# Layer 0's later modulation starts with the mLSTM's weights; each half's sum is taken ahead of the next half

## The chip, the core and the metric

The kernel runs on one core of a Trainium2 chip. The metric is the device time of one execution in microseconds; before the change it is 1823.27 us, the median of three runs. The core's engines are named as the profile names them: PE is TensorE's matrix multiply, PEld its weight load, DVE VectorE, ACT ScalarE, POOL GpSimd, SP SyncE, whose queue issues the loads.

## What is computed

Two layers of a diffusion trunk on 256 latent tokens and 256 context tokens of width 1024. In each layer an adaLN modulation (six vectors of 1024 per side, from `SiLU(c)` and `SiLU(c_ctx)`) acts on the normed input; one projection feeds four mixers side by side (A: HGRN2 recurrence, B: mLSTM, C: grouped-query attention, D: latent attention); their outputs are gated, summed, projected out and added; then comes a squared-ReLU MLP, modulated too. Cut to that:

```python
for l in range(DEPTH):
    mod = jnp.split((s_c @ w_ada[l] + b_ada[l])[:, None, :], 6, axis=-1)
    mod_c = jnp.split(s_cc @ w_ada[l][:, :n_cm * D_MODEL] + b_ada[l][:n_cm * D_MODEL], n_cm)
    h_l = modulate(rms_norm(x_l, g_norm1[l]), mod[0], mod[1])       # h_c with mod_c
    p_l = h_l @ w_in[l]
    ...   # ya: hgrn2, yb: mlstm, yc: gqa, yd: mla, latent reads context too
    x_l = x_l + mod[2] * (merge_branches((ya_l, yb_l, yc_l, yd_l), lat['gates'], w_branch[l]) @ w_out[l])
    x_l = x_l + mod[5] * squared_relu_mlp(modulate(rms_norm(x_l, g_norm2[l]), mod[3], mod[4]), w_ff1[l], w_ff2[l])
    ...   # the context side likewise in layer 0
return rms_norm(x_l, g_final)
```

## The kernel before

**Weights.** Every big weight comes in blocks of 128 x 1024 f32 (512 KB). `plan` writes a list of them (`specs`) in the order of use; `get` hands out the next and, by `_prep`, loads and splits one block ahead. A block is loaded into one of three buffers (`raw`), then ScalarE writes its rounded high part (`whi`, line 139) and VectorE the rest (`wlo`, line 140), each from a pool of two. A product takes three matmuls, high by high, high by low, low by high; a block is 24 matmuls of 512 columns. They go into PSUM tiles `pd`. All other matmuls, those of the recurrences and attentions, go into four PSUM buffers `pm`.

**Modulation.** The first two of layer 0's six vectors are made at the start (`ada_start`, names `ad`). The other four are two groups of 2048 columns (`ada_specs(0, 1)` and `(0, 2)`), each in two halves of eight blocks: 32 chunks. A chunk is not split. VectorE multiplies it by the side's conditioning value and adds it to an accumulator of 128 x 1024, once for each of the two sides (lines 390 and 392). After the eighth chunk of a half, `ada_sum` sums the accumulators over partitions with matmuls (line 404), copies the row (line 407, ScalarE), transposes it (line 263) and adds the bias (line 414). It is called at the next `get` of a split block at which the half is one block old, or at once with `now=True`; `mixer_b` has such a call ahead of its state C. The accumulators, C, the attentions' probabilities and queries share the pool `w4` of four buffers of 4 KB per partition.

**What sets the order.** `fill` holds the chunks that wait; `plan` puts one behind each split block while there are any. `ORDER[0]` sets the units: `A` (three weights for each of three heads, the first head's come at the start), `RA` (A's readout, 4 blocks), `B` (12 blocks; `mixer_b` makes gates and state), `b` (one mLSTM head of one side; four context heads, then four latent ones), `M0` (a quarter of a branch merge, 3 blocks), `CD` (queries for C and D, 6 blocks), `RB`, `C`, and so on. A scheduler then sets each engine's queue, by priority in the order of the program, as buffers come free. A queue runs in order.

**The recurrences.** A head of A has eight levels: ScalarE copies K, TensorE multiplies (line 636), VectorE multiplies K and Q by F (lines 654, 658), F by itself (662) and picks results (663). A head of B: scores (line 865), then for each of two directions a row matmul (870), VectorE (876, 879), ScalarE's exponential (881) and decay (889), VectorE (882, 883, 890), the product with values and state (900); then the norm (904 to 906) and the output (909, 910). Behind and between these stand the matmuls of weight blocks, named filling below.

Of the kernel before, what the change touches and what calls it, by code (L numbers as in the profile page):

```python
# [40 lines left out]
class Trunk:  # L41
# [337 lines left out]
    def ada_chunk(self, key):  # L379

        nc = self.nc
        _, l, g, k, jj = key
        raw, _ = self.get(key)
        sides = (0, 1) if l == 0 or g == 0 else (0,)
        if k == 0:
            self.ada_acc = [self.t("w4", [128, 1024], name=f"aacc{g}{jj}{r}") for r in sides]
        for r in sides:
            acc, s = self.ada_acc[r], self.scol[:, k, r:r + 1]
            if k == 0:
                nc.vector.tensor_scalar(out=acc, in0=raw, scalar1=s, scalar2=None, op0=ALU.mult)  # L390
            else:
                nc.vector.scalar_tensor_tensor(out=acc, in0=raw, scalar=s, in1=acc, op0=ALU.mult, op1=ALU.add)  # L392
        if k == KT - 1:
            self.pending = (l, g, jj, sides, self.ada_acc, self.next_use + 1)
# [632 lines left out]
    def mixer_c(self, l):  # L1027
        nc = self.nc
        need = l == 0
        i0 = 0 if need else 2  # L1030
        q0 = i0 * 128
        KVD, QS, R = self.KVD, self.QS, self.CDR
        kn = self.t("w2", [128, 4, 128], name=f"ckn{l}")
        for i in range(4):
            kv = kn[:, i, :].rearrange("p (h c) -> p h c", h=2)
            nc.vector.scalar_tensor_tensor(out=kv, in0=KVD[:, i, 16:144].rearrange("p (h c) -> p h c", h=2), scalar=0.125,
                                           in1=R[:, i, 8:10].unsqueeze(2).to_broadcast([128, 2, 64]), op0=ALU.mult, op1=ALU.mult)
            if i < 2:
                nc.vector.tensor_tensor(out=kv, in0=kv, in1=self.gain[:, l * 2 + 1, :].unsqueeze(1).to_broadcast([128, 2, 64]), op=ALU.mult)
            else:  # L1040
                tmp = self.t("w2", [128, 512])[:, 0:128].rearrange("p (h c) -> p h c", h=2)
                self.rope(tmp, kv, self.rt[:, l * 2 + 1, 0, i - 2, :], self.rt[:, l * 2 + 1, 1, i - 2, :], 2, nc.vector)
                nc.vector.tensor_scalar(out=kv, in0=tmp, scalar1=1.0, scalar2=None, op0=ALU.mult)
        for i in range(i0, 4):
            qv = QS[:, i, :].rearrange("p (h c) -> p h c", h=8)
            nc.vector.tensor_tensor(out=qv, in0=qv, in1=R[:, i, 0:8].unsqueeze(2).to_broadcast([128, 8, 64]), op=ALU.mult)
            if i < 2:
                nc.vector.tensor_tensor(out=qv, in0=qv, in1=self.gain[:, l * 2, :].unsqueeze(1).to_broadcast([128, 8, 64]), op=ALU.mult)
            else:
                tmp = self.t("w2", [128, 512])  # L1050
                self.rope(tmp.rearrange("p (h c) -> p h c", h=8), qv, self.rt[:, l * 2, 0, i - 2, :], self.rt[:, l * 2, 1, i - 2, :], 8, nc.vector)
                nc.vector.tensor_copy(QS[:, i, :], tmp)
        ps = self.pm()
        for i in range(4):
            self.tr(ps[:, i * 128:(i + 1) * 128], kn[:, i, :])
        ks = [self.dup_key(ps, g * 64, f"ck{l}{g}") for g in range(2)]
        Y = self.t("b16", [128, 2, 4, 512], F32R, name=f"yc{l}")
        yield Y
        for pp in range(2):
            Ts = []  # L1060
            for kvh in range(2):
                ps = self.pm()
                for i in range(i0, 4):
                    c0 = (kvh * 4 + pp * 2) * 64
                    self.tr(ps[:, i * 128:(i + 1) * 128], QS[:, i, c0:c0 + 128])
                Ts.append(self.split_pair(ps, q0))
            for gg in range(2):
                g4 = pp * 2 + gg
                pts = {}
                for sd in range(i0 // 2, 2):  # L1070
                    ns = 256 if sd == 0 else 512
                    for kvh in range(2):
                        PT = pts[kvh, sd] = self.t("w4", [128, 4, 256])
                        for tt in range(2):
                            i = 2 * sd + tt
                            pss = self.pm()
                            self.score64(pss[:, 0:ns], Ts[kvh][gg], slice(i * 128, (i + 1) * 128), ks[kvh], ns, True, True)
                            self.softmax_t(pss[:, 0:ns], ns, PT[:, 0:ns // 128, tt * 128:(tt + 1) * 128])

                def values(g4=g4, pts=pts):  # L1080
                    po = self.pm()
                    for sd in range(i0 // 2, 2):
                        nst = 2 if sd == 0 else 4
                        for st in range(nst):
                            for kvh in range(2):
                                nc.tensor.matmul(po[kvh * 64:(kvh + 1) * 64, sd * 256:(sd + 1) * 256],  # L1086
                                                 KVD[:, st, 144 + kvh * 64:144 + (kvh + 1) * 64], pts[kvh, sd][:, st, :],
                                                 start=(st == 0), stop=(st == nst - 1), skip_group_check=True)
                    nc.scalar.activation(out=Y[:, 0, g4, q0:], in_=po[:, q0:], func=AF.Copy)
                    nc.vector.tensor_tensor(out=Y[:, 1, g4, q0:], in0=po[:, q0:], in1=Y[:, 0, g4, q0:].bitcast(F32), op=ALU.subtract)  # L1090

                self.later.append((0, values))
                if g4 == 3:
                    self.run_later()
                yield
# [263 lines left out]
    def run(self):  # L1359
        nc = self.nc  # L1360
        for l in range(2):
            if l == 0:
                self.plan_start()
                self.fill += self.ada_specs(0, 1) + self.ada_specs(0, 2)
            m = [0] * 4
            for u in ORDER[l].split():
                if u == "A":
                    self.plan_a(l)
                elif u == "RA":
                    self.plan_tmw(("ag", l), l, O_AG)  # L1370
                elif u == "B":
                    self.plan_b(l)
                elif u == "CD":
                    self.plan_cd(l)
                elif u == "RB":
                    self.plan_tmw(("bo", l), l, O_BO)
                elif u[0] == "M":
                    r = int(u[1])
                    self.plan_merge(l, r, (m[r],))
                    m[r] += 1  # L1380
            self.plan_out(l)
            if l == 0:
                self.fill += self.ada_specs(1, 0) + self.ada_specs(1, 1) + self.ada_specs(1, 2)
            self.plan_ff(l)
# [136 lines left out]
```

## Time and profile before

| | |
|---|---|
| median of 3 runs | 1823.27 us (1821.34 to 1823.35) |
| the profiled execution | 1824.29 us, its span 1822.5 us |
| TensorE busy | 1772.4 us, 97% |
| VectorE busy | 1201.3 us, 66% |
| ScalarE busy | 834.6 us, 46% |
| loads | 228.80 MB, mean 129 GB/s |

A record of a matmul lasts from its start to a modelled end, and the next starts well before that end; so the spacing of starts tells TensorE's rate, and idle time is what lies between one record's end and the next start. The granted clock (PEclk) is a share of 2.4 GHz. A row of the timeline may merge equal instructions, with their count behind x; in brackets stands the idle time of the engine just before, and what ended it. A matmul of plain f32 operands shows as two records.

### The profile page before, as it was taken

Reading aid. Unit: us, or ns where it says so; the run is one execution under the profiler, and the core shown is the slowest. Engines: PE = TensorE matmul, PEld = TensorE weight load, DVE = VectorE, ACT = ScalarE, POOL = GpSimd, SP = SyncE. Lnnn points to the kernel's source line nnn. Section 1 sums busy time; section 2 is a strip of 40 time slices with the busy share of each in tenths; the row PEclk is TensorE's granted clock in tenths of the full one; section 3 lists DMA queues with packets and bytes.
Section 4 is the critical chain, followed back from the end, with each engine's and each line's share of the span. In section 5 each row is a group of like instructions: output and inputs, shape, how many; then the busy total and the mean of one; then the engine's idle time right before and its main releaser. Section 6 shows DMA issues by size and latency. Waiting matters only on the chain.

```text
span 1822.5 us, 26354 instructions
## 1 busy us (share of the span) xinstructions
PE 1772.4 (97%) x10214; PEld 1496.8 (82%) x10214; DVE 1201.3 (66%) x2047; ACT 834.6 (46%) x1481; POOL 122.3 (7%) x139
## 2 busy tenths in 40 slices
PE   7999899999999999999999999999999999989998
PEld 5788777888767778897888888888789779989998
DVE  5798798647754444579884435587666965656665
ACT  4443343354653333443433334443455664545555
POOL 0000000000001111010101010000000001001110
PEclk9999899999999999999999999999999999999999
DMA  9643245223112234337783234222335425545554
GB/s 292 195 122 107 70 139 178 86 87 93 47 36 77 73 120 123 105 114 222 242 288 105 93 95 145 72 74 62 93 116 168 139 70 151 156 134 160 181 183 137
DMA packets 210045, 234.71 MB, mean 129 GB/s; under 512 B 8320, under 2 KB 186880, under 8 KB 209664
## 3 DMA queue, kind: packets, MB, share of 16 engines
q1 hardware_dynamic: 209920, 233.03, 42.2%
q8 instruction: 80, 1.31, 0.3%
q14 instruction: 45, 0.37, 0.1%
HBM read 228.80 MB, written 4.19 MB: 128 GB/s over the span
## 4 chain that ended last, share of the span: by engine, by line
PE 83%; DVE 9%; issue 3%; ACT 3%; DMA 2%; SPq 0%; POOL 0%; ACTq 0%; DVEq 0%; POOLq 0%
PE pd L198 14%; PE pd L196 14%; PE pd L197 14%; PE pd L168 4%; PE pd L167 4%; PE pd L169 4%; PE pd L238 3%; PE pd L239 3%; PE pd L240 3%; PE pm L263 3%; PE pm L636 2%; DVE wlo L140 2%; PE pm L900 1%; DVE aacc L392 1%; PE pm L1086 1%
## 5 line engine op out<-in xcount | busy, mean ns | idle before, releaser
L140 DVE TENSOR_TENSOR wlo<-raw,whi 128x1024 fp32r<-128x1024 f32 (+1 forms) x305 | 384.7, 1262 | 275.9 <-ACT whi L139 273.8
L139 ACT ACTIVATE whi<-raw 128x1024 fp32r<-128x1024 f32 (+1 forms) x305 | 321.6, 1056 | 401.6 <-PE pd L197 180.4
L198 PE MATMUL pd<-HH,wlo 128*128 128x256 f32 (+1 forms) x1104 | 371.2, 337 | 2.7 <-DVE wlo L140 2.6
L196 PE MATMUL pd<-HH,whi 128*128 128x256 f32 (+1 forms) x1104 | 372.1, 337 | 0.0
L197 PE MATMUL pd<-HL,whi 128*128 128x256 f32 (+1 forms) x1104 | 370.2, 335 | 0.0
L198 PEld LDWEIGHTS pd<-HH,wlo 128*128 128x128 f32 x1104 | 209.4, 190 | 25.3 <-DVE wlo L140 4.9
L196 PEld LDWEIGHTS pd<-HH,whi 128*128 128x128 f32 x1104 | 209.5, 190 | 22.0 <-issue 1.5
L197 PEld LDWEIGHTS pd<-HL,whi 128*128 128x128 f32 x1104 | 209.6, 190 | 20.3 <-issue 0.5
L196 PE MATMUL pd<-b,whi 128*128 128x256 f32 (+1 forms) x528 | 175.5, 332 | 0.0
L198 PE MATMUL pd<-b,wlo 128*128 128x256 f32 (+1 forms) x528 | 175.2, 332 | 0.2 <-DVE wlo L140 0.2
L197 PE MATMUL pd<-b,whi 128*128 128x256 f32 (+1 forms) x528 | 175.4, 332 | 0.0
L238 PE MATMUL pd<-whi,HH 128*128 128x512 f32 (+1 forms) x272 | 107.9, 397 | 2.3 <-DVE d L712 1.0
L196 PEld LDWEIGHTS pd<-b,whi 128*128 128x128 f32 x528 | 100.3, 190 | 10.5 <-issue 0.8
L198 PEld LDWEIGHTS pd<-b,wlo 128*128 128x128 f32 x528 | 100.3, 190 | 10.3 <-DVE wlo L140 1.0
L197 PEld LDWEIGHTS pd<-b,whi 128*128 128x128 f32 x528 | 100.3, 190 | 9.4 <-DVE b L1347 0.2
L239 PE MATMUL pd<-whi,HL 128*128 128x512 f32 (+1 forms) x272 | 106.4, 391 | 0.0
L240 PE MATMUL pd<-wlo,HH 128*128 128x512 f32 (+1 forms) x272 | 104.4, 391 | 0.5 <-DVE wlo L140 0.5
L434 ACT ACTIVATE w<-X 128x256 f32<-128x256 f32 x120 | 47.5, 411 | 104.4 <-DVE X L1243 104.4
L169 PE MATMUL pd<-HH,wlo 128*128 128x512 f32 (+1 forms) x232 | 87.6, 378 | 4.6 <-DVE wlo L140 4.6
L1236 POOL TENSOR_TENSOR mg<-mg,d 128x512 f32<-128x512 f32 (+1 forms) x48 | 53.4, 1114 | 555.4 <-DVE d L1235 540.4
L1346 POOL TENSOR_TENSOR d<-d 128x256 f32<-128x256 f32 (+1 forms) x60 | 56.5, 946 | 492.6 <-ACT b L1344 477.8
L168 PE MATMUL pd<-HL,whi 128*128 128x512 f32 (+1 forms) x232 | 87.6, 377 | 0.0
(422 smaller groups left out, 3306.8 us busy)
## 6 DMA issues: line engine op xcount, KB each, us to landing
raw<-in_w_in_dram SPq DMA_DIRECT2D x140, 512.0 KB, 3.7
raw<-in_w_ff_dram SPq DMA_DIRECT2D x128, 512.0 KB, 3.7
w<-in_w_ada_dram SPq DMA_DIRECT2D x48, 512.0 KB, 5.0
raw<-in_w_ada_dram SPq DMA_DIRECT2D x32, 512.0 KB, 3.8
raw<-in_w_branch_dram SPq DMA_DIRECT2D x24, 512.0 KB, 3.5
raw<-in_w_out_dram SPq DMA_DIRECT2D x16, 512.0 KB, 3.5
w<-in_w_ada_dram SPq DMA_DIRECT2D x28, 256.0 KB, 5.5
raw<-in_w_branch_dram SPq DMA_DIRECT2D x16, 256.0 KB, 4.0
```

The costliest lines, as they stand in the source:

```text
L139: nc.scalar.activation(out=hi[:, 0:n], in_=raw[:, 0:n], func=AF.Copy)
L140: nc.vector.tensor_tensor(out=lo[:, 0:n], in0=raw[:, 0:n], in1=hi[:, 0:n].bitcast(F32), op=ALU.subtract)
L167: nc.tensor.matmul(out, lh, rh, start=(i == 0), stop=False)
L168: nc.tensor.matmul(out, lh, rl, start=False, stop=False)
L169: nc.tensor.matmul(out, ll, rh, start=False, stop=(i == n - 1))
L196: nc.tensor.matmul(o, wh, act[0], start=(k == 0), stop=False, skip_group_check=True)
L197: nc.tensor.matmul(o, wh, act[1], start=False, stop=False, skip_group_check=True)
L198: nc.tensor.matmul(o, wl, act[0], start=False, stop=(k == KT - 1), skip_group_check=True)
L238: nc.tensor.matmul(o, hh, wh, start=(k == 0), stop=False, skip_group_check=True)
L239: nc.tensor.matmul(o, hl, wh, start=False, stop=False, skip_group_check=True)
L240: nc.tensor.matmul(o, hh, wl, start=False, stop=(k == KT - 1), skip_group_check=True)
L1346: eng.tensor_tensor(out=r, in0=r, in1=r, op=ALU.mult)
```

## The change

The 32 chunks of layer 0 are put on `fill` ahead of unit `B` and no longer ahead of unit `A`. So A's nine weight blocks and RA's four have no chunk between them, and the chunks stand behind the blocks of B, of three quarters of the merge, of CD and of RB. At the first chunk of a half `ada_sum(True)` now takes the sum of the half before, and so does the head of `mixer_c`.

```diff
@@ -383,6 +383,7 @@
         if k == 0:
+            self.ada_sum(True)
             self.ada_acc = [self.t("w4", [128, 1024], name=f"aacc{g}{jj}{r}") for r in sides]
@@ -1030,6 +1031,7 @@
         KVD, QS, R = self.KVD, self.QS, self.CDR
+        self.ada_sum(True)
         kn = self.t("w2", [128, 4, 128], name=f"ckn{l}")
@@ -1361,7 +1363,6 @@
             if l == 0:
                 self.plan_start()
-                self.fill += self.ada_specs(0, 1) + self.ada_specs(0, 2)
             m = [0] * 4
@@ -1369,6 +1370,9 @@
                 elif u == "B":
+                    if l == 0:
+
+                        self.fill += self.ada_specs(0, 1) + self.ada_specs(0, 2)
                     self.plan_b(l)
```

Line numbers of the changed kernel are one higher behind line 385, two higher behind line 1033.

VectorE's queue in the first head of A, before (`ah` is the head's K, Q and F, `w2` the result, `aacc` an accumulator, `raw30` a chunk):

```order
L392 SCALAR_TENSOR_TENSOR aacc100_814<-raw30_1038,scol_112,aacc100_814 128x1024
L654 TENSOR_TENSOR ah00_680<-ah00_680 128x2x64x4
L658 TENSOR_TENSOR ah00_680<-ah00_680 128x2x64x4
L663 COPY_PREDICATED w2_96_690<-lmask_647,pm_100_719 128x512
L662 TENSOR_TENSOR ah00_680<-ah00_680 128x128
L140 TENSOR_TENSOR wlo29_888<-raw29_885,whi29_887 128x1024
L654 TENSOR_TENSOR ah00_680<-ah00_680 128x2x32x8
L658 TENSOR_TENSOR ah00_680<-ah00_680 128x2x32x8
L663 COPY_PREDICATED w2_96_690<-lmask_647,pm_101_729 128x512
L662 TENSOR_TENSOR ah00_680<-ah00_680 128x64
L392 SCALAR_TENSOR_TENSOR aacc101_815<-raw30_1038,scol_112,aacc101_815 128x1024
```

The same levels after:

```order
L655 TENSOR_TENSOR ah00_680<-ah00_680 128x2x64x4
L659 TENSOR_TENSOR ah00_680<-ah00_680 128x2x64x4
L663 TENSOR_TENSOR ah00_680<-ah00_680 128x128
L655 TENSOR_TENSOR ah00_680<-ah00_680 128x2x32x8
L659 TENSOR_TENSOR ah00_680<-ah00_680 128x2x32x8
L664 COPY_PREDICATED w2_96_690<-lmask_647,pm_101_729 128x512
L663 TENSOR_TENSOR ah00_680<-ah00_680 128x64
L140 TENSOR_TENSOR wlo26_876<-raw26_873,whi26_875 128x1024
```

The sums over chunks are gone from between the levels, and weights are split less far ahead. The first chunk's sum (L391) now stands in the fourth head.

TensorE's queue in the mLSTM's latent heads, from one direction's product to the next head's row matmul, before (`pm` are PSUM tiles of the recurrence, `pd` of the weights, `C0` the state):

```order
L900 MATMUL pm_314_2654<-bv0_2119,w2_312_2644 128x129 x2
L865 MATMUL pm_316_2669<-w2_232_2095,w2_226_2009 128x256
L900 MATMUL pm_314_2654<-C0_2288,w2_313_2650 128x129
L900 MATMUL pm_314_2654<-bv0_2119,w2_312_2644 128x129
L900 MATMUL pm_314_2654<-C0_2288,w2_313_2650 128x129
L865 MATMUL pm_316_2669<-w2_232_2095,w2_226_2009 128x256
L870 MATMUL pm_317_2672<-nM0_1908,rsel_101 128x256
L198 MATMUL pd_343_2878<-HH_125,wlo87_2884 128x512
L196 MATMUL pd_343_2878<-HH_125,whi87_2883 128x512
L197 MATMUL pd_343_2878<-HL_126,whi87_2883 128x512
```

After, from the row matmul of the third latent head on:

```order
L871 MATMUL pm_307_2584<-nM0_1836,rsel_101 128x256
L901 MATMUL pm_310_2596<-bv0_2031,w2_308_2586 128x129
L871 MATMUL pm_311_2602<-nM0_1836,rsel_101 128x256
L901 MATMUL pm_310_2596<-C0_2200,w2_309_2592 128x129
L901 MATMUL pm_310_2596<-bv0_2031,w2_308_2586 128x129 x2
L901 MATMUL pm_310_2596<-C0_2200,w2_309_2592 128x129
L901 MATMUL pm_314_2614<-bv0_2031,w2_312_2604 128x129
L866 MATMUL pm_316_2629<-w2_222_2007,w2_216_1921 128x256
L901 MATMUL pm_314_2614<-bv0_2031,w2_312_2604 128x129
L901 MATMUL pm_314_2614<-C0_2200,w2_313_2610 128x129
```

Before, 19 such matmuls on weights follow the row matmul shown, and 24 stand within each latent head; after, six stand in the second latent head and none from there to the end of the fourth. Weights follow behind it, six blocks in a row.

VectorE's queue at the end of the fourth latent head, after (`bden` is the head's norm, `bh0` its output, `mod0` the modulation):

```order
L891 TENSOR_TENSOR w2_323_2658<-w2_323_2658,w2_222_2007 64x256
L391 TENSOR_SCALAR aacc201_2738<-raw69_2713,scol_112 128x1024
L906 TENSOR_TENSOR bden_325_2668<-bden_325_2668,bEM_228_2026 128x4
L393 SCALAR_TENSOR_TENSOR aacc201_2738<-raw71_2769,scol_112,aacc201_2738 128x1024
L907 RECIPROCAL bden_325_2668<-bden_325_2668 128x4
L415 TENSOR_TENSOR mod0_103<-pm_330_2732,PT_107 128x2x4 x2
L1235 SCALAR_TENSOR_TENSOR mg0_2300<-d2_333_2765,pd_335_2779 128x512
L911 SCALAR_TENSOR_TENSOR bh0_2227<-pm_324_2662,bden_325_2668,bh0_2227 128x128 x2
L1235 SCALAR_TENSOR_TENSOR mg0_2300<-d2_334_2767,pd_336_2793 128x512
L393 SCALAR_TENSOR_TENSOR aacc201_2738<-raw73_2809,scol_112,aacc201_2738 128x1024
L699 TENSOR_REDUCE cdst_356_3203<-w2_359_3211 128x4
L140 TENSOR_TENSOR wlo74_2814<-raw74_2811,whi74_2813 128x1024
```

The last group's second accumulator (`aacc201`) is first written here, some 80 rows behind its first (`aacc200`), from the chunks `raw69`, `raw71` and `raw73`; the next weight split is `wlo74`. Before, the accumulators of every half are written side by side.

## Rows read from the trace of the kernel before

**Rows 1.** The page's head: span, and each engine's busy time.
```profile
span 1822.5 us, 26354 instructions
PE 1772.4 (97%) x10214; PEld 1496.8 (82%) x10214; DVE 1201.3 (66%) x2047; ACT 834.6 (46%) x1481; POOL 122.3 (7%) x139
```

**Rows 2.** Stretches: length, busy us (instructions) by engine, PEclk, loads' share, GB/s.
```profile
core 0: us, PE busy (x) PEld busy (x) DVE busy (x) ACT busy (x) POOL busy (x), PEclk, DMA share, GB/s
160.00:180.00 20.00, 18.64 (x116) 15.99 (x115) 16.89 (x25) 7.39 (x12) 0.59 (x2) 1.00 0.32 95
180.00:200.00 20.00, 15.98 (x92) 13.28 (x90) 20.00 (x32) 5.68 (x9) 0.00 (x0) 0.95 0.36 106
200.00:220.00 20.00, 16.38 (x91) 14.34 (x92) 12.76 (x23) 8.79 (x15) 1.57 (x3) 0.79 0.24 73
...
240.00:260.00 20.00, 17.33 (x76) 13.39 (x75) 19.65 (x32) 9.17 (x13) 0.00 (x0) 1.00 0.31 91
...
280.00:300.00 20.00, 18.60 (x117) 13.48 (x117) 15.29 (x24) 6.98 (x12) 0.00 (x0) 1.00 0.63 186
...
400.00:420.00 20.00, 20.00 (x106) 17.21 (x105) 14.78 (x36) 12.79 (x30) 0.00 (x0) 1.00 0.35 104
...
1220.00:1240.00 20.00, 19.86 (x125) 17.20 (x124) 16.94 (x37) 8.02 (x17) 1.15 (x2) 1.00 0.26 71
```

**Rows 3.** Eight stretches from 60 to 220 us, instructions on accumulators alone, summed.
```profile
sum 160.00, PE 1.07 PEld 0.42 DVE 39.56; mean PE 0.13 PEld 0.05 DVE 4.94
```

**Rows 4.** Line 392, layer 0: count, shortest, median and longest ns, first and last.
```profile
L392 DVE SCALAR_TENSOR_TENSOR aacc<-raw,scol,aacc x56: 1265/1276/1292, 72.2 to 325.7; 128x1024 f32<-128x1024 f32 x56
```

**Rows 5.** Timeline of TensorE, end of HGRN2's last head: start, us, instruction, idle before.
```profile
193.90 1.16 PE L636 MATMUL pm<-ah 128*128 128x128 f32 x8 [1.35 <-ACT ah L632]
196.44 1.16 PE L645 MATMUL pm<-ah 128*128 128x128 f32 x8 [1.38 <-DVE ah L658]
198.67 1.11 PE L263 MATMUL pm<-cst,ah 128*128 128x128 f32 x4 [1.07 <-DVE ah L654]
...
209.61 0.44 PE L263 MATMUL pm<-cst,arow 128*128 128x128 f32 x2 [2.17 <-ACT arow L407]
```

**Rows 6.** Stretches ahead of and in the first fall of the clock, columns as in rows 2.
```profile
189.60:196.40 6.80, 4.11 (x25) 3.20 (x24) 6.80 (x13) 2.13 (x3) 0.00 (x0) 1.00 0.29 78
196.40:203.20 6.80, 5.01 (x25) 4.42 (x26) 4.94 (x7) 1.58 (x3) 0.53 (x1) 0.63 0.56 167
```

**Rows 7.** Timeline of TensorE in the second latent head of the mLSTM.
```profile
345.58 0.38 PE L870 MATMUL pm<-nM,rsel 100*128 100x256 f32 x1
345.80 0.39 PE L198 MATMUL pd<-HH,wlo 128*128 128x512 f32 x1
346.03 0.40 PE L196 MATMUL pd<-HH,whi 128*128 128x512 f32 x1
...
350.38 0.36 PE L870 MATMUL pm<-nM,rsel 100*128 100x256 f32 x1
...
352.72 0.61 PE L900 MATMUL pm<-bv,w 128*128 128x129 f32 x4
...
355.37 0.39 PE L870 MATMUL pm<-nM,rsel 100*128 100x256 f32 x1
```

**Rows 8.** Timeline of VectorE in that head.
```profile
350.79 0.48 DVE L876 SCALAR_TENSOR_TENSOR w<-pm,U,cst 128x256 f32<-128x256 f32 x1
...
352.12 0.42 DVE L882 TENSOR_TENSOR w<-w,pm 128x256 f32<-128x256 f32 x1 [0.59 <-ACT w L881]
...
356.20 0.60 DVE L910 SCALAR_TENSOR_TENSOR bh<-pm,bden,bh 128x128 f32<-128x128 f32 x2
```

**Rows 9.** The page: splitting (busy, mean ns, idle before), and a chunk's load (KB, us).
```profile
L140 DVE TENSOR_TENSOR wlo<-raw,whi 128x1024 fp32r<-128x1024 f32 (+1 forms) x305 | 384.7, 1262 | 275.9 <-ACT whi L139 273.8
L139 ACT ACTIVATE whi<-raw 128x1024 fp32r<-128x1024 f32 (+1 forms) x305 | 321.6, 1056 | 401.6 <-PE pd L197 180.4
...
raw<-in_w_ada_dram SPq DMA_DIRECT2D x32, 512.0 KB, 3.8
```

## The prediction

> **What bounds the kernel now.** I read the busy line first: TensorE 1772.4 of 1822.5 us, VectorE 1201.3 [rows 1]. TensorE is the bound, so only what opens or closes holes in its queue can move the time. The stretches of 20 us say where the holes are [rows 2]: none to speak of at 400, but 1.36, 4.02 and 3.62 us between 160 and 220, where the first layer's HGRN2 ends. VectorE is full there (20.00 of 20 from 180 to 200), and 39.56 us of its work between 60 and 220 are modulation sums [rows 3], 1.276 us each [rows 4]. The rows of TensorE show it waiting for VectorE and ScalarE at every step of the last head, 1.35, 1.38 and 1.07 us, and then for the modulation's own row, 2.17 us [rows 5]. The clock falls to its lower level, 1.2 GHz, just behind that [rows 6]. The same recurrence in layer 1, without modulation sums beside it, leaves TensorE idle for 0.14 us in 20 [rows 2].
>
> **What the change removes.** The 32 chunks start with the mLSTM's weights, so 13 of them (9 behind head weights, 4 behind the readout's) leave the HGRN2 stretch, and those that followed slide down by 13 weights. That is 13 × 2 × 1.276 = 33 us of VectorE work; in the new order four sums are left ahead of the last head's end. What that is worth is not 33 us but the holes of TensorE: 1.36 + 4.02 + 3.62 = 9.0 us idle [rows 2]. A gap hides a little more, as a record lasts 0.39 us where the next matmul could start 0.23 us later [rows 7]: nine gaps by 0.16 us, 1.4 us. The clock stood at 0.95 and 0.79 of full speed in two stretches of 20 us [rows 2], 1.0 + 4.2 = 5.2 us of pulses, of which about 1 us fell into idle time: 4.2 us. Sum 14.6 us. Some of it stays: the new order has levels of the recurrence with only 4 or 5 filling matmuls (about 1 us), where VectorE's two multiplies barely fit. Layer 1, by 0.14 us in 20, says 1 us for the whole stretch; I leave 2.5 us. **Gain: 12 us** (9 to 15).
>
> **What it adds: a stretch without filling.** The mLSTM recurrence is a chain, and in the old order TensorE fills its waits with weight matmuls, 24 for each head of the latent side. The accumulators come from a pool of four buffers. In the new order the chunks of the last group begin while the recurrence runs: its state C and the two sums of the half before hold three buffers, the first accumulator takes the fourth, and the second finds none. It waits until that half's sum has run, and this sum stands in TensorE's queue behind the last head. So three chunks sit in all three load buffers, no further weight can be loaded, and after the last weight that was split in time TensorE's queue holds six filling matmuls and then none for the rest of three heads.
>
> The price from the rows of one head. Direction two is a chain that I can read whole: its row matmul L870 starts at 350.38, VectorE answers at 350.79, ScalarE's exponential lets VectorE go on at 352.12, L900 starts at 352.72 and the next head's L870 at 355.37 [rows 7, 8]: 4.99 us. Direction one has the same 2.34 us to its first L900, the 0.60 us of L910 that VectorE does in between [rows 8], and 0.22 us to the next L870: 3.16 us. A bare head takes 8.1 us. With filling it took 9.79 us (345.58 to 355.37), of which 24 × 0.2275 = 5.46 us were filling, so its own matmuls are 4.33 us. TensorE idles 8.1 − 4.3 = 3.8 us per head; three heads are 11.4, less 1.4 us for the six filling matmuls, plus 0.7 us for the modulation's row at the end, which nothing covers now: **loss 10.7 us** (7.5 to 13). The filling itself is not lost; it runs later, all of it.
>
> **Restart.** When the buffers come free, the next weight has to be loaded (3.8 us as the chunks take), split (1.06 and 1.26 us) and stands behind a sum of 1.28 us [rows 4, 9]: 7.4 us. One split weight is waiting for TensorE, 24 × 0.2275 = 5.5 us, and the sum with its row takes about 1 us: **1 us** of hole (0 to 2). Loads queued on SP behind that weight are the following weights and chunks, already in this sum.
>
> **Chunks behind the recurrence.** Thirteen chunks, and half of the three that waited, now stand beside the weights of the branch merge, the attention queries and the mLSTM readout, where there were none and TensorE had no hole (20.00 at 400). Per weight VectorE then does 1.26 + 2 × 1.276 = 3.8 us for 5.5 us of TensorE, so on the mean it keeps up. The nearest rows, twelve weights with twelve chunks, have holes of 2.67 and 1.40 us [rows 2], but there with the gates' scans on a full VectorE. **2 us** (0 to 4).
>
> **The clock in the bare stretch.** TensorE would work about 14 of 25 us there. Just ahead of the first fall in the old trace it was as thinly busy, 4.11 of 6.80 us, and after it the clock stood at 1.2 GHz for most of a stretch of the same length [rows 6]. So I expect one fall or two. The two of the old trace cost 4.2 us together, by the working above; here a part lies in the chain's waits: **3 us** (0 to 6).
>
> **Nothing.** The ten sums of accumulators, each now taken ahead of the next half, keep their instructions; outside the bare stretch TensorE has weights queued around them, so 0 (±1 us). The six of layer 1 stand beside the feed-forward, whose order changes in nothing else. From the mLSTM readout's last weights on, TensorE's order in layer 0 is the old one up to the feed-forward.
>
> The sum is −12 + 10.7 + 1 + 2 + 3 = +4.7 us. It is made on the profiled execution (1824.29 us, span 1822.5), which lies 0.06% over the median of 1823.27. I predict **1828.0 us**.
>
> **Rivals.** *The clock holds, and the later chunks are hidden.* The bare stretch stays at 2.4 GHz and VectorE keeps up: −12 + 10.7 + 1 = 0 to +2, **1824.5 us**, no difference. For it: layer 1's recurrences and attention keep the full clock. Against it: rows 6. The Trainium skill ("TensorE: Matmul & The Clock Gate", "Why this matters for your kernels") ties a fall to a long pause between bursts of matmuls; by that rule the pauses of some 2.3 us here might leave the clock up and the sum would be +1.7. The trace disagrees: the longest pause ahead of the first fall was 1.38 us.
>
> *Faster: the bare heads run shorter.* The one mechanism is the chain's length. VectorE and ScalarE do nothing but the recurrence there, and if a head takes 6 us rather than 8.1, the three cost 3 × 1.7 − 1.4 + 0.7 = 4.4 us, the clock stays up, and −12 + 4.4 + 1 + 1 gives −5.6: **1817.7 us**. The point from which it decides is a head of about 6.4 us. For it: the old rows have filling matmuls in the queue that may delay the chain. Against it: the chain of direction two has waits on other engines from end to end, and its 4.99 us cannot hide much.
>
> *Slower by far.* The clock falls for several stretches, the holes beside the late chunks come as in the gates' stretch, and HGRN2 gives back only 9 us because its levels wait on the short filling: −9 + 12 + 2 + 4 + 6 = +15, **1838 us**.
>
> That the change does not move the chunks is ruled out by the order.
>
> **How the numbers follow.** About 0.2% (3.6 us) can be told from no change. Forecast 0.42; no difference 0.27; faster 0.17; slower by far 0.14. So faster 0.17, same 0.27, slower 0.56. The bounds of the terms lie at −15 + 7.5 = −7.5 and −9 + 13 + 2 + 4 + 6 = +16, and 1 us on either side for the sums. All ends hardly meet; the range is cut by little at each end: 1817 to 1837 us.
>
> **What would show it.** Right: between 80 and 200 us VectorE is no longer full and TensorE has under 3 us of idle time up to the HGRN2 readout, with the clock at 1.00; the latent heads' L871 stand some 8 us apart in pairs of 3 and 5; the first write of the last group's second accumulator follows the sum L405, with about 11 us of TensorE idle ahead of it; a lower clock in that stretch. Wrong: heads at 6 us, a clock at 1.00 throughout, or holes of the old size in the HGRN2 stretch, which would mean that its own chain and not the sums held TensorE.

## The result and the profile after

The changed kernel takes 1832.19 us (median; 1828.52 to 1835.04) against 1822.30 us for the kernel before on the same chip: a ratio of 1.0054, with a 95% interval of 1.0038 to 1.0070, so 9.9 us slower. The profiled execution of the changed kernel took 1835.04 us; it has this page head (to be read against [rows 1]):

```profile
span 1833.3 us, 26367 instructions
PE 1780.9 (97%) x10214; PEld 1498.5 (82%) x10214; DVE 1204.8 (66%) x2047; ACT 834.7 (46%) x1481; POOL 122.7 (7%) x139
```

The stretches of 20 us of the changed kernel, with the columns of [rows 2] (busy time and count for PE, PEld, DVE, ACT and POOL, then the granted clock, the DMA share and GB/s):

```profile
160.00:180.00 20.00, 19.75 (x123) 16.63 (x122) 15.19 (x24) 7.96 (x14) 0.59 (x2) 1.00 0.18 51
180.00:200.00 20.00, 20.00 (x118) 17.01 (x117) 15.83 (x26) 10.28 (x17) 1.58 (x3) 1.00 0.34 101
200.00:220.00 20.00, 19.18 (x97) 16.54 (x96) 17.45 (x23) 8.30 (x11) 0.00 (x0) 1.00 0.43 121
220.00:240.00 20.00, 15.90 (x71) 12.67 (x70) 17.65 (x29) 10.73 (x14) 0.00 (x0) 0.97 0.40 114
240.00:260.00 20.00, 20.00 (x89) 14.82 (x89) 18.57 (x29) 7.22 (x13) 0.00 (x0) 0.86 0.44 132
...
320.00:340.00 20.00, 15.76 (x82) 11.80 (x83) 13.20 (x37) 6.95 (x20) 1.52 (x5) 1.00 0.09 26
340.00:360.00 20.00, 15.47 (x64) 10.37 (x64) 9.71 (x28) 6.47 (x17) 0.30 (x1) 0.57 0.05 11
360.00:380.00 20.00, 20.00 (x90) 16.53 (x89) 18.50 (x21) 7.70 (x14) 0.00 (x0) 1.00 0.72 223
```

Against [rows 2] the holes of HGRN2's end are gone: TensorE idles 0.25, 0.00 and 0.82 us from 160 to 220, where it had idled 1.36, 4.02 and 3.62 us, VectorE is down from 20.00 to 15.83 us between 180 and 200, and the clock stays up. From 320 to 360 a new hole has opened, 4.24 and 4.53 us, with hardly any transfers (26 and 11 GB/s) and the clock at 0.57 of full speed. At 360 the load queue starts again (223 GB/s).

To put one number on each stretch I use the **lost time**: for each matmul the time from its start to the next one's start, less the median of that for its line and shape; the remainders of more than 20 ns are summed over a stretch. It holds idle time and lower clock together. It is worked out from all TensorE rows of one profiled execution of each kernel.

| stretch, us | before | changed | difference | prediction |
|---|---|---|---|---|
| 60 to 220 (HGRN2) | 24.9 | 13.8 | -11.1 | -12 |
| 220 to 320 (mLSTM gates, context heads) | 10.0 | 10.8 | +0.8 | 0 |
| 320 to 380 (latent heads) | 3.0 | 19.7 | +16.7 | +10.7 +1 +3 |
| 380 to 460 (behind the recurrence) | 1.5 | 4.4 | +2.9 | +2 |
| all the rest | 90.6 | 92.7 | +2.1 | 0 (+-1) |
| whole | 130.0 | 141.4 | +11.4 | +4.7 |

The two profiled executions differ by 10.75 us, which the lost times account for within 0.7 us.

The latent heads in TensorE's rows of the changed kernel (start, duration, operation, and in brackets the idle time ahead with what ended it), to be read against [rows 7]:

```profile
328.47 0.38 PE L871 MATMUL pm<-nM,rsel 100*128 100x256 f32 x1
...
331.31 0.46 PE L901 MATMUL pm<-bv,w 128*128 128x129 f32 x2 [1.07 <-DVE w L883]
331.52 0.36 PE L871 MATMUL pm<-nM,rsel 100*128 100x256 f32 x1
...
336.49 0.39 PE L871 MATMUL pm<-nM,rsel 100*128 100x256 f32 x1
339.33 0.46 PE L901 MATMUL pm<-bv,w 128*128 128x129 f32 x2 [2.46 <-DVE w L883]
339.55 0.36 PE L871 MATMUL pm<-nM,rsel 100*128 100x256 f32 x1
...
346.93 0.58 PE L871 MATMUL pm<-nM,rsel 100*128 100x256 f32 x1
349.96 0.77 PE L901 MATMUL pm<-bv,w 128*128 128x129 f32 x2 [2.46 <-DVE w L883]
350.38 0.56 PE L871 MATMUL pm<-nM,rsel 100*128 100x256 f32 x1
...
356.47 0.64 PE L901 MATMUL pm<-C,w 128*128 128x129 f32 x2
357.04 1.64 PE L405 MATMUL pm<-aacc,selr 128*32 128x256 f32 x14
359.18 0.44 PE L263 MATMUL pm<-cst,arow 128*128 128x128 f32 x2 [0.50 <-ACT arow L408]
359.66 0.50 PE L196 MATMUL pd<-HH,whi 128*128 128x512 f32 x1
```

The reader sees the pairs of 3 and 5 us that the prediction named: 328.47, 331.52, 336.49, a head of 8.02 us at full clock (its first 3.05 us hold the six filling matmuls; the same step of the bare third head, from 336.49 to 339.55, takes 3.06 us). From 336.49 to the next pair at 346.93 it takes 10.44 us; the clock falls in between. The weight's matmul L196 follows 0.48 us behind the row's transposes. The clock around it, in three pieces of the same view:

```profile
334.00:341.00 7.00, 4.53 (x26) 3.15 (x25) 3.62 (x12) 1.82 (x6) 0.61 (x2) 1.00 0.01 2
341.20:348.00 6.80, 5.62 (x15) 3.58 (x15) 1.74 (x7) 1.39 (x6) 0.20 (x1) 0.50 0.00 0
348.00:358.20 10.20, 7.62 (x34) 5.50 (x37) 5.77 (x17) 3.48 (x8) 0.00 (x0) 0.50 0.00 2
```

It stands at 1.2 GHz (0.50) from 341.2 to 358.2, some 17 us in one piece.

VectorE's first write of the last group's second accumulator:

```profile
357.14 0.75 DVE L391 TENSOR_SCALAR aacc<-raw,scol 128x1024 f32<-128x1024 f32 x1 [3.25 <-PE pm L901]
```

It comes 0.03 us behind the end of the last product that reads the state C (L901, 356.47 to 357.11), while the sum L405 is still running (to 358.68).

### The profile page after: what moved, and what is told of

Same layout as the page of the kernel before. It is cut to its first block, busy times and chain, and to the rows that moved or that the text cites. A ratio compares the mean times of both kernels' runs of the same rounds, so it can differ in the third digit from the quotient of the medians.

```text
span 1833.3 us, 26367 instructions
## 1 busy us (share of the span) xinstructions
PE 1780.9 (97%) x10214; PEld 1498.5 (82%) x10214; DVE 1204.8 (66%) x2047; ACT 834.7 (46%) x1481; POOL 122.7 (7%) x139
## 4 chain that ended last, share of the span: by engine, by line
PE 85%; DVE 7%; ACT 3%; DMA 2%; issue 2%; SPq 0%; POOL 0%; ACTq 0%; DVEq 0%; POOLq 0%
PE pd L198 14%; PE pd L196 14%; PE pd L197 14%; PE pd L169 4%; PE pd L167 4%; PE pd L168 4%; PE pd L240 4%; PE pd L238 4%; PE pd L239 4%; PE pm L637 3%; PE pm L263 2%; DVE wlo L140 2%; PE pm L901 1%; PE pm L1088 1%; DMA raw<-in_w_ada_dram 1%
## 5 line engine op out<-in xcount | busy, mean ns | idle before, releaser
L196 PE MATMUL pd<-HH,whi 128*128 128x256 f32 (+1 forms) x1104 | 373.1, 338 | 0.1
L196 PEld LDWEIGHTS pd<-HH,whi 128*128 128x128 f32 x1104 | 210.2, 190 | 21.9 <-issue 1.2
L196 PE MATMUL pd<-b,whi 128*128 128x256 f32 (+1 forms) x528 | 175.8, 333 | 0.0
L198 PEld LDWEIGHTS pd<-b,wlo 128*128 128x128 f32 x528 | 100.4, 190 | 10.7 <-DVE wlo L140 1.3
L196 PEld LDWEIGHTS pd<-b,whi 128*128 128x128 f32 x528 | 100.4, 190 | 10.3 <-issue 0.8
L167 PE MATMUL pd<-HH,whi 128*128 128x512 f32 (+1 forms) x232 | 89.0, 383 | 0.5 <-ACT whi L139 0.5
```

The source lines that it names most:

```text
L167: nc.tensor.matmul(out, lh, rh, start=(i == 0), stop=False)
L196: nc.tensor.matmul(o, wh, act[0], start=(k == 0), stop=False, skip_group_check=True)
L198: nc.tensor.matmul(o, wl, act[0], start=False, stop=(k == KT - 1), skip_group_check=True)
```

## The experiments

**What was open.** The prediction had one cause for the bare stretch: the second accumulator of the last group finds no buffer (**theory A**). TensorE's order shows a second candidate (**theory B**). The sum of the half before asks for a PSUM buffer of the pool that the heads use in turn, and so it stands behind the last head. Its row `arow` is a buffer of the pool `d2`, from which the branch merge takes its tanh's, L1225, too. In ScalarE's order of the changed kernel the merge's next two tanh's stand right behind that row:

```profile
358.74 0.38 ACT L408 ACTIVATE arow<-pm 128x256 f32<-128x256 f32 x1 [1.42 <-PE pm L405]
359.02 1.08 ACT L1225 ACTIVATE d<-pd 128x512 f32<-128x512 f32 x2
```

Until they run, the merge's PSUM pairs are occupied, and a weight that is loaded and split can't be used. The third possibility was that the moved chunks themselves cost the time (**theory C**). Every ratio below is to the kernel before, timed beside the run on the same chip.

How many filling matmuls stand in TensorE's order in each of the eight gaps from one latent row matmul (L870, L871) to the next, beginning in front of the first (so the kernel before has 23, 24 and 27 in its first three latent heads):

| kernel | filling matmuls, gap by gap |
|---|---|
| before | 15, 18, 5, 19, 5, 19, 8, 17 |
| changed | 9, 14, 5, 6, 0, 0, 0, 0 |
| state elsewhere | 14, 12, 0, 0, 0, 0, 0, 0 |
| row elsewhere | 9, 14, 6, 12, 5, 12, 0, 0 |
| start only | 9, 14, 6, 12, 5, 12, 0, 0 |
| both elsewhere | 14, 16, 10, 22, 13, 15, 10, 15 |

**The state C in another pool.**

```diff
-        C = self.t("w4", [128, 2, 2, 129], name=f"C{l}")
+        C = self.t("w4" if l else "p2", [128, 2, 2, 129], name=f"C{l}")
```

> The changed kernel with the first layer's mLSTM state C in the softmax's pool, which is unused there, so that the last group's second accumulator has a buffer while the recurrence runs. Theory A (that of the prediction: the full pool of accumulators empties TensorE's queue): the latent heads are filled again, the 16.7 us lost between 320 and 380 us mostly come back, 1816 to 1820 us. Theory B (the sum of the half before stands behind the last head because it wants one of the PSUM buffers that the heads take in turn; its row arow has its place in the pool of the merge's tanh, and no tanh after it can be written before it; so the merge's PSUM pairs stay occupied and no weight can be used): the accumulators are not what is waited for, all four latent heads stay without filling, one more than in the changed kernel, though the same filling now runs earlier: 1830 to 1840 us. Theory C (the chunks beside the recurrence and behind it load VectorE, and this costs): about as the changed kernel, 1832 us.

Measured: 1843.05 us, a ratio of 1.0111 (1.0095 to 1.0128), slower than the changed kernel. Theory A falls as the sole cause; B named the direction and fell 3 us short. VectorE's rows also say what the second accumulator had waited for: with C in another pool it is written at 300.61, right behind the first (299.87), while the row of the half before comes only at 366.52. The buffer that it lacked was C's, and it did not wait for the sum. The stretches:

```profile
320.00:340.00 20.00, 15.65 (x70) 11.56 (x69) 17.03 (x38) 6.45 (x18) 1.53 (x5) 0.78 0.34 105
340.00:360.00 20.00, 14.84 (x47) 10.74 (x48) 8.66 (x27) 5.66 (x16) 0.61 (x2) 0.50 0.09 28
360.00:380.00 20.00, 18.74 (x87) 14.10 (x87) 7.56 (x18) 7.88 (x18) 0.00 (x0) 0.86 0.09 27
```

The lost time from 320 to 380 is 27.2 us (19.7 in the changed kernel): the second latent head is bare as well, and the clock is down for longer. Another 8.9 us went between 380 and 460, where a wait of 3.8 us for a weight's low half is followed by another fall of the clock.

**The row in a buffer of its own.**

```diff
-            row = self.t("d2", [128, 512], name=f"arow{l}{g}{jj}")[:, 0:256]
+            row = self.sm([128, 256], "arow", 1)
```

> The changed kernel with the sum's row arow in a buffer of its own instead of the pool of the merge's tanh; C and the accumulators stay as they are. Theory A: the second accumulator is still refused a buffer, all load buffers are full, so three heads stay bare: 1832 us. Theory B: the tanh's no longer stand behind the row, and two of the three bare heads have weights again; one bare head is left (3.8 us, with the row 4.5) where the accumulator is still waited for, and the long stretch at 1.2 GHz between 341 and 358 us goes: 1819 to 1824 us. Theory C: 1832 us, since the chunks stand where they stood.

Measured: 1831.07 us, 1.0051 (1.0038 to 1.0064). By the time A and C (1832 us) fit, and B, which asked for 1819 to 1824, missed; by the trace it is neither A nor B alone. From 320 to 340 TensorE is busy for 19.05 us, so two heads have their filling back, as B said. But the loss has moved, as the stretch and the waits show:

```profile
340.00:360.00 20.00, 12.61 (x57) 8.41 (x56) 12.19 (x28) 7.98 (x20) 0.00 (x0) 0.71 0.28 80
PE pm L901 <- DVE w L883: 4.0, 3, 2.5
PE pd L196 <- ACT whi L139: 3.8, 1, 3.8
```

One head is bare, the clock falls, and then TensorE waits 3.8 us for a weight that could not be loaded sooner, because the chunks still held the load buffers for the missing accumulator (the weight's load is issued at 352.70, behind that accumulator's first write at 351.92). In the changed kernel that wait was not there: its next weight was already split and stood waiting for PSUM. The lost time from 320 to 380 is 17.2 us.

**Both edits together.**

> The changed kernel with both edits: the sum's row in a buffer of its own, and C in the softmax's pool. Theories A and B: no bare head but the last, the gain of 11 us in HGRN2's stretch stands against 2.9 us behind the recurrence and a fall of the clock of 3.4 us at 239: 1814 to 1819 us, faster than the kernel before. Theory C: 1828 to 1832 us, since all the chunks still stand beside the recurrence.

Measured: 1816.27 us, 0.9967 (0.9955 to 0.9979), faster than the kernel before. The stretches that were bare:

```profile
320.00:340.00 20.00, 20.00 (x108) 16.74 (x106) 17.02 (x35) 9.18 (x20) 1.23 (x4) 1.00 0.40 116
340.00:360.00 20.00, 20.00 (x104) 16.04 (x104) 17.71 (x39) 8.88 (x21) 0.61 (x2) 1.00 0.40 125
360.00:380.00 20.00, 20.00 (x122) 15.53 (x121) 13.55 (x24) 9.17 (x18) 0.00 (x0) 1.00 0.60 184
```

TensorE is full at full clock, with the chunks beside the recurrence and with more VectorE work in these 60 us than in the changed kernel (48.3 us against 41.4). No head is bare, the last one neither. That rules theory C out for the bare stretch; behind the recurrence the chunks do cost (5.3 us lost from 380 to 460, where the kernel before loses 1.5). There are two walls, each of them enough to empty the queue; taking one away shows the other (**theory D**).

**The later start without the early sums.**

```diff
         if k == 0:
-            self.ada_sum(True)
...
-        self.ada_sum(True)
         kn = self.t("w2", [128, 4, 128], name=f"ckn{l}")
```

> The changed kernel without its two early sums: the modulation begins with the mLSTM's weights, and each half is summed where the kernel before did it. Theory A: the second accumulator waits as it does in the changed kernel, three bare heads, 1832 us. Theory B: the row now stands behind the tanh's of the second merge step, and two of the three heads have filling (in TensorE's order 14, 6, 12, 5, 12, 0, 0 filling matmuls from row matmul to row matmul, against 14, 5, 6, 0, 0, 0, 0): one bare head, 1819 to 1824 us, so that the early sums, costed at 0 +- 1 in the prediction, would be what costs most. Theory C: 1832 us.

Measured: 1829.98 us, 1.0041 (1.0029 to 1.0054); B, with 1819 to 1824 us, missed again. The order is that of the row elsewhere, and so is the loss: 17.3 us from 320 to 380, with a wait of 3.4 us for the weight. So without the early sum the row is no wall, but the accumulator is. The difference of 2.2 us to the changed kernel lies within the intervals.

**The early sums without the later start.** The two lines above, put into the kernel before:

> The kernel before with the two early sums alone, its modulation beginning where it did. Theory D: the sums cost only where one of them stands behind the recurrence, which is not so here (group one is summed ahead of it, and the filling of the heads is the old one in TensorE's order): 0 +- 1 us, 1822 to 1824. Rival: a sum ahead of the next half holds TensorE up each time by its row's trip through ScalarE, some 0.5 us at ten places: 1827 us.

Measured: 1823.07 us, 0.9999 (0.9989 to 1.0008). They change nothing in the time there; what they change in the order is told below, with the row alone.

**The buffers in the kernel before, and the later start with the buffers but without the early sums.** These complete the square.

> The kernel before (modulation beginning with the recurrence's weights, sums where they were) with the two buffers moved as in the kernel with both: the row arow in a buffer of its own, C in the softmax's pool. Theory D (the buffers are worth something only where the sum of a half stands behind the recurrence): the filling of the heads is unchanged in TensorE's order, 0 +- 1 us, 1822 to 1825. Rival (the buffers bring a gain by themselves, and the gain of the kernel with both is theirs): 1816 to 1819 us.

> The changed kernel without its early sums, but with both buffers moved: the later start and the buffers alone. Theory D: TensorE's order has the same filling in every head as with the early sums, so the gain is the later start's and the early sums bring nothing: 1815 to 1818 us. Rival (the early sums free the accumulators sooner and are needed for the gain): one bare head as in the changed kernel without early sums, 1822 to 1830 us.

Measured: 1819.83 and 1818.17 us.

| ratio to the kernel before | old buffers | both moved |
|---|---|---|
| old start, old sums | 1 | 0.9977 (0.9968 to 0.9987) |
| old start, early sums | 0.9999 (0.9989 to 1.0008) | not run |
| later start, old sums | 1.0041 (1.0029 to 1.0054) | 0.9972 (0.9961 to 0.9983) |
| later start, early sums | 1.0054 (1.0038 to 1.0070) | 0.9967 (0.9955 to 0.9979) |

Theory D missed the first of the two: the buffers bring 3.6 us even with the old start. For the second it held in that the early sums are not needed (0.2 us above its range), but not in that the gain is the later start's. What I had not expected stands between the two cells: with both buffers moved, the later start itself can't be told from nothing. The lost times say why: from 60 to 220 it gains 7.4 us (21.2 to 13.8), from 380 to 460 it loses 6.0 (1.6 to 7.6). The profiled executions, 1821.78 and 1818.07 us, lie further apart than the medians, by another 1.9 us gained from 220 to 320. The later start's row from 380 to 400, 2.71 us idle, and the wait that makes it:

```profile
380.00:400.00 20.00, 17.29 (x117) 15.75 (x116) 12.47 (x19) 9.84 (x27) 0.00 (x0) 0.98 0.41 128
PE pd L198 <- DVE wlo L140: 2.7, 1, 2.7
```

**The row alone, in the kernel before.** Why do the buffers help there?

> The kernel before with the sum's row arow alone in a buffer of its own. Both buffers together were worth 4 us there, against the expectation. Theory F (the same wall stands in the kernel before, at HGRN2's end: the row of the first half is in the pool of the readout's activations L709, which in ScalarE's order stand behind it and hold TensorE's PSUM): all of the gain is the row's, 1818.5 to 1821 us. Rival (the state C holds an accumulator's buffer): 1823 to 1824 us.

Measured: 1820.21 us, 0.9981 (0.9971 to 0.9991). Within the intervals the row has all of it. ScalarE's rows of the kernel before at HGRN2's end, where L407 writes the row and L709 is the tanh of the readout, which takes its product out of PSUM:

```profile
209.19 0.36 ACT L407 ACTIVATE arow<-pm 128x256 f32<-128x256 f32 x1
209.46 1.56 ACT L709 ACTIVATE d<-pd 128x512 f32<-128x512 f32 x3
```

and of that kernel with the row elsewhere (rows of other lines between them left out):

```profile
186.28 0.60 ACT L709 ACTIVATE d<-pd 128x512 f32<-128x512 f32 x1 [1.51 <-PE pd L240]
187.64 0.60 ACT L709 ACTIVATE d<-pd 128x512 f32<-128x512 f32 x1 [0.24 <-PE pd L240]
190.04 0.60 ACT L709 ACTIVATE d<-pd 128x512 f32<-128x512 f32 x1
...
205.51 0.36 ACT L407 ACTIVATE arow<-pm 128x256 f32<-128x256 f32 x1
```

It is the same wall in another place: three L709 run 20 us earlier once the row does not stand ahead of them. Of the hole, a good part only moves: TensorE is full between 180 and 200, and then waits 6.3 us for the readout's product. That the row has the gain is shown; that it comes by these three is not, and the early sums alone speak against it. In that kernel the same three tanh's (there L710) run as early, at 186.44, 187.81 and 190.45, and TensorE is as full from 180 to 200, yet the time is that of the kernel before (0.9999). Its wait for the readout's product is longer, as the rows of the row alone and of the early sums alone show:

```profile
PE pm L263 <- DVE ao L713: 6.3, 1, 6.3
PE pm L263 <- DVE ao L714: 8.9, 1, 8.9
```

What makes the second longer is open.

**Where the chunks start.** Three more kernels move the start. The first begins with the readout's first weight and leaves the buffers alone; the second has both buffers moved as well; the third begins with the readout's third weight, both buffers moved. The edit of the third (the other two have the filling's line ahead of one undivided readout):

```diff
                 elif u == "RA":
-                    self.plan_tmw(("ag", l), l, O_AG)
+                    self.plan_tmw(("ag", l), l, O_AG, quarters=(0, 1))
+                    if l == 0:
+                        self.fill += self.ada_specs(0, 1) + self.ada_specs(0, 2)
+                    self.plan_tmw(("ag", l), l, O_AG, quarters=(2, 3))
                 elif u == "B":
-                    if l == 0:
-
-                        self.fill += self.ada_specs(0, 1) + self.ada_specs(0, 2)
                     self.plan_b(l)
```

> The changed kernel with the modulation beginning four weights earlier, with the HGRN2 readout's, and nothing else: group one then ends with the mLSTM's own weights, its last half is summed ahead of the recurrence (C's early sum), and neither the row nor the accumulators are waited for while the heads run; in TensorE's order 8 to 16 filling matmuls stand between the row matmuls of every head. Theory D (two walls, the row's place behind the heads and the accumulator's buffer, each enough to empty the queue): with both gone by timing alone, 1814 to 1820 us, as with both buffers moved. Theory C' (it is the chunks ahead of the gates and beside HGRN2's end that cost, not the walls): four chunks return to HGRN2's end, and 1821 to 1824 us, the kernel before.

> The start with the HGRN2 readout's weights, and the row and C in buffers of their own as well. Theory D: no wall is left to take away, so the two pools bring nothing beyond the earlier start: the time of the start at the readout alone, within 2 us, 1813 to 1819. Rival: the walls still cost in part there (accumulators held by C): 3 to 5 us faster than the earlier start alone.

> Both buffers moved and the early sums kept, with the modulation beginning at the third weight of the HGRN2 readout. The start with the mLSTM's weights loses 5.3 us between 380 and 460 us, the start with the readout's first weight 4.8 us between 200 and 220 us. Theory (each chunk that leaves one crowded stretch of VectorE joins the other): between the two, 1814 to 1817 us, no better than either. Rival (two chunks fewer in both take the worst waits from both): 1810 to 1813 us.

Measured: 1814.96 us, 0.9960 (0.9947 to 0.9972); 1816.30 us, 0.9968 (0.9956 to 0.9979); 1814.75 us, 0.9949 (0.9936 to 0.9962). The first confirms theory D by timing alone: with group one complete ahead of the recurrence, no buffer needs to move, and the buffers add nothing to it. The third has the lowest time of all. Its losses are 14.3 us from 60 to 220 and 3.9 from 380 to 460, against 16.1 and 3.4 of the first, and 13.2 and 5.3 of the kernel with both buffers moved: between the two, as the first expectation had it, and not better than the first beyond the intervals. These versions beat the kernel before and the changed one.

**No chunk at the gates.** This kernel is the last one, with one edit more, so the two are compared:

```diff
+        fill, self.fill = self.fill, []
         self.plan_tmw(("kv", l), l, O_KV0, w=464)
+        self.fill = fill
```

> As the kernel with both buffers moved, but with no chunk behind the four weights of the mLSTM's gates and keys; the chunks begin two weights before the readout's end instead. The stretch from 220 to 240 us has 4.7 us lost there: a wait of 2.8 us for the low half of a weight (wlo), which stands behind chunk sums and the gates' scans on VectorE, and a fall of the clock behind it. Theory E (the chunk sums delay the scans and with them the weight): the wait shrinks under 1 us, the clock stays up, 1811 to 1814 us. Rival (the scans alone hold the weight up, as they did before with 2.0 us): as with both buffers moved, 1815 to 1817 us.

Measured: 1818.56 us, 0.9977 (0.9968 to 0.9986). Theory E asked for 1811 to 1814 us and its rival for 1815 to 1817, so both missed. TensorE's longest wait from 60 to 420 us:

```profile
PE pd L169 <- DVE wlo L140: 4.1, 1, 4.1
```

It is slower than the kernel with the chunks at the gates (0.9949). The wait there is 4.1 us, where that kernel has 2.4 us as its longest and the one with both buffers moved 2.8. But the edit did not take the chunk sums away from the gates. VectorE's rows ahead of the weight (left out between them: the gates' scans L789 and L790; L791 takes their result):

```profile
228.83 2.48 DVE L393 SCALAR_TENSOR_TENSOR aacc<-raw,scol,aacc 128x1024 f32<-128x1024 f32 x2 [2.37 <-DMA raw<-in_w_ada_dram]
231.23 0.68 DVE L782 SCALAR_TENSOR_TENSOR w<-w,w 36x512 f32<-36x512 f32 x1
...
236.05 0.67 DVE L791 TENSOR_TENSOR w<-pm,w 36x512 f32<-36x512 f32 x1
236.65 1.21 DVE L140 TENSOR_TENSOR wlo<-raw,whi 128x1024 fp32r<-128x1024 f32 x1
```

The input of L782 was ready at 228.54, with the end of ScalarE's L781; two sums of one chunk, 2.48 us, stand between. So the run does not decide theory E: the weight waits behind 5.4 us of work with the gates' scans in it and behind the sums, and no run here takes either away. A second wait, 3.4 us between 380 and 420, lies behind the recurrence, where the postponed chunks now end.

## Why the prediction was right, and where it was not

The direction was right and 1832.19 us lies inside the range, but the size was half of what came: 4.7 us forecast, 9.9 measured. By the steps of the sum:

- **What it removes** was read rightly: 12 us forecast, 11.1 measured, and TensorE has 1.07 us of idle time from 160 to 220 where the test asked for under 3.
- **The bare stretch**: the price of a head was right (8.1 us forecast, 8.02 measured at full clock), and so was their number. The cause was half of it. The step "the second finds none", with the full load buffers, is true. The next, "It waits until that half's sum has run", is not: it waits for C, which the last head still reads (first write at 357.14, ahead of the sum's end at 358.68; with C elsewhere at 300.61), so that sign of the prediction did not come. And the accumulator was not enough by itself, nor was it needed: alone it leaves one bare head and a wait of 3.4 to 3.8 us, and with its buffer free the stretch became longer, 1843.05 us. What I had not looked at is the row's place in `d2` behind the last head, which alone holds the queue empty. That the forecast of three bare heads came out right on the accumulator alone was luck.
- **Restart**, 1 us: there was none to speak of, 0.48 us from the transposes to L196, because the weight had been split already. It is there, 3.4 to 3.8 us, as soon as the accumulator is the only wall.
- **The clock in the bare stretch** is the term that was mis-sized: 3 us forecast, for one fall or two. The clock fell once and stayed down for 17 us. The head at 336.49 took 10.44 us instead of 8.02, and the last, from 346.93 to 357.04, 10.11: 2.4 and 2.1 us, 4.5 us without what the sum and the row lose. With the step above, 14.7 us were forecast for the stretch and 16.7 came. TensorE's idle time itself was 8.77 us from 320 to 360, where about 11 was asked for: at 1.2 GHz the same matmuls fill more of the waits.
- **Chunks behind the recurrence**: 2 us forecast, 2.9 measured, inside 0 to 4. With the bare stretch gone it costs more, 3.8 us with both buffers moved and 6.1 without the early sums.
- **Not in the sum** was the wait for a weight's low half at the mLSTM's gates, 3.6 us up to 239.55, in the end of which the clock fell, from 238.8 to 245.6 us. The net of that stretch is only +0.8 us, since other waits there went.
- **A reading**: rows 6 have the first fall of the clock ahead of the wait for the row at 209.61 [rows 5] and not behind it; no term of the sum rests on that.
- **Nothing** for the sums: right in the kernel before by the time (0.9999), though its hole moves. In the changed kernel one of them is part of the wall, which the ratios alone can't show (1.0054 and 1.0041); the orders do.

Of the rivals, the one in which the clock holds had the Trainium skill's rule beside it ("TensorE: Matmul & The Clock Gate", "Why this matters for your kernels"), which ties a fall to a long pause between bursts of matmuls. The trace disagrees with it again: between the clock's rise at 245.6 and the fall at 341.2 the longest pause was 2.46 us. The fall at 238.8, with a pause of 3.6 us, agrees with it. The rival "slower by far" had 6 us for the clock, as far above the 4.5 as the forecast lay below; its holes in HGRN2 did not come. "Bare heads run shorter" fell with 8.02 us.

## What to carry to other kernels

When work is moved past a loop, list every buffer that its last step takes, PSUM and the small rows too, and ask of each pool who else allocates from it behind that step: a buffer that is taken in program order can hold up an unrelated stage. A stretch can have two walls, each hiding the other, so that taking one away shows no gain; try the pair before giving the idea up. And where a filling is moved out of one crowded stretch, price the stretch that takes it in by the kernel in which nothing else waits: here 6.0 of the 7.4 us gained at one end were lost again at the other.

## What was not expected of the hardware

One fall of the clock lasted 17 us, though its pauses (0.90, 2.46 and 0.62 us) were no longer than those ahead of it: TensorE was busy for 5.62 of 6.80 and 7.62 of 10.20 us at 1.2 GHz, since the same matmuls then take longer (the pair of L866 1.22 us instead of 0.70), and the clock rose only at 358.2, among the sum's matmuls that end the stretch. And in a pause of 3.6 us at the gates the clock fell in the changed kernel, where the kernel before, with one of 2.0 us, kept the clock.
